# A decoder step on one core: operations re-ordered at six places, last sums and one evacuation split

## The chip, the cores and the metric

The kernel runs on one core of a Trainium2 chip. The metric is device microseconds of one execution. The engines are named as the profile names them: PE is TensorE (matmul), PEld its weight loads, DVE is VectorE, ACT is ScalarE, POOL is GpSimd, SP is SyncE, which issues most DMAs.

## The reference

One inference step of a hybrid decoder layer for 512 prompt rows and 64 sample rows (8 samples of 8 rows), all of width 1024, in float32:

```python
u = rms(x) * g_pre_mix;  proj = u @ w_in          # z, xbc, dt, q, k, v, ig, fg, og
xbc = silu(causal_conv(xbc, conv_w));  dt = softplus(dt + bias)
y = ssd_scan(xs, dt, a, bm, cm, h0)               # Mamba-2 heads, chunks, cumulative sums, exp
h = mlstm_scan(q, k, v, ig, logf, c0, n0, m0)     # stabilised mLSTM heads
x = x + rms(concat(y_gated, h_gated) @ w_out) * g_post_mix
x = x + rms(cross_attention(rms(x) * g_pre_x, mem_k, mem_v) @ w_xo) * g_post_x
u = rms(x) * g_pre_ffn
x = x + rms((silu(u @ w_gate) * (u @ w_up)) @ w_down) * g_post_ffn
```

It also returns the memory's keys and values, and the new states of the convolution, the SSM and the mLSTM for both groups.

## The kernel before, in words

The activations are kept transposed, features on the 128 partitions, the T = 576 rows of both groups in the free dimension. Most products are made in three matmuls: weights and activations are each split into a high part (a cast to a shorter float) and a low part (the rest), and `gemm` (L201 to L212) issues for each block k of 128 features high x high (L208), high weights x low activations (L209) and low weights x high activations (L211). A tile of output has two halves (`HALVES`: 256 and 320 columns). Weights come in by DMA as 128x1024 floats (`split_w`, L178): ScalarE casts the high part, VectorE subtracts it for the low part, or ScalarE writes the negated high part and a GpSimd DMA adds the original on top.

The work goes through stages. (1) The input projection, 36 tiles of weights; tiles 1 to 12 feed the convolution, and between them VectorE and ScalarE work on the gates' rows (`r1`, `r2`: cumulated logs, maxima), which PE turns into columns with ten small transposes (L586 to L594), copied by ScalarE to `CT` (L591, L595); two products with `CT` follow (L597, L604). (2) The SSD scan (`ssd_prompt`): per pair of heads two decay matrices, each made by a product (L669), additions on VectorE (L672), an exponential on ScalarE (L674, collected in `exps`, 16 in all) and a product on VectorE (L675), then 16 small matmuls (L682). PE's time is filled with the mLSTM's values (`values`, L840 on): two groups of two heads, whose last chunk of 64 sample rows is stacked on both halves of the partitions, copied by ScalarE (L877), summed by VectorE (L878) and scaled by ScalarE (L879). Then come the mLSTM scan, the output gates, and the output projection. (3) Cross-attention, and its output projection `xo` (L1539 on): tiles 0, 1 and 2 are computed around the last head, with their evacuation (a square for the norm, L270, and a scaled copy, L1560, both on ScalarE) kept back until tile 3's weights have been cast. The three PSUM banks of the pool `g` rotate: tile 3 takes that of tile 0. (4) The feed-forward part, with seven products in place of eight for each 2x2 block of weights and rows (`Seven`, `Pair` for gate and up, `Down`): VectorE builds sums and differences of weight tiles in `sw` and others, and `parts2` (L1867) casts the sum `sw` to high and low. `Down` (768 columns of weights, eight of them in two groups) accumulates on `f2`. (5) A last chunk of six blocks of the down projection without that scheme (`down_chunk`, `w_of`, L2158): second halves of all eight output tiles (order 6, 7, 0, 1, ... 5), where the first three start with four blocks while the last gate products are still being made (`last.late()`, products L1935, cast to `hh` and `hl` by `Plain.put`, L2138). (6) The end (L2178 on): the eight first halves, six steps each, with the second half's norm and output beside them; then squares, sums over features by products with a column of ones (`root`, L2181), a root on ScalarE, transposes of the result to token rows (`f_rows`), and the last additions and stores.

What sets the order: in most of the kernel a build-time scheduler orders the instructions of each engine by priority (`tc.high_priority`) and by a simulated timeline (`schedule_with_timeline_sim`, L113); `tc.issue_after(x)` makes the instructions of the block that run on the engine of `x` come behind `x` in that engine's queue, without a semaphore. From the attention's output projection to the first pair, and at the end, the order is written out: `at_(p, fn)` puts a step at place p, and `tc.manual_schedule` issues the steps sorted by place. At the end, half-tile step k of tile j stands at j + k/6, its evacuation `evac0` at j + 1.03, the transposes of tile rows at 7.35 and 8.2, the sums `root` at 8.4, the last transposes at 8.7. Engines run their own queue in order; SP's queue issues loads in order, each waiting for its buffer (`raw` has two buffers in the pool `weights`, `rawx` two in the pool `ffn`).

Of the kernel before, what the change touches and what calls it, by code (L numbers as in the profile page):

```python
# [11 lines left out]
F32 = mybir.dt.float32  # L12
F32R = mybir.dt.float32r
BF16 = mybir.dt.bfloat16
AF = mybir.ActivationFunctionType
# [100 lines left out]
def build(nc, tc, ctx, I, O):  # L116
# [52 lines left out]

    loads, casts, accs = [], [], []  # L170

# [5 lines left out]

    def split_w(src, n=1024, cut=CUT, acc=False, pool=None, to=None, raw=None):  # L178
# [7 lines left out]
        casts.append(A.copy(hi[:, :n], raw[:, :n]))  # L186
        for e, a, b in ((V, 0, cut), (G, cut, n)):
            if b > a and e is G and acc:

                A.activation(lo[:, a:b], hi[:, a:b].bitcast(F32), AF.Copy, scale=-1.0)  # L190
                accs.append(G.dma_start(lo[:, a:b], src[:, a:b], accum_op=ALU.add))  # L191
            elif b > a:
                e.tensor_tensor(lo[:, a:b], raw[:, a:b], hi[:, a:b].bitcast(F32), op=ALU.subtract)  # L193
        return hi, lo

    def split(hi, lo, src, eng=None, cast=None):
        c = (cast or A.copy)(hi, src)  # L197
        (eng or V).tensor_tensor(lo, src, hi.bitcast(F32), op=ALU.subtract)  # L198
        return c

    def gemm(ps, units, xh, xl, t0, n, k0=0, k1=None, order=None, late=0):  # L201


        tiles = [(hi[:, j * P:(j + 1) * P], lo[:, j * P:(j + 1) * P]) for hi, lo, nk in units for j in range(nk)]
        order = order or range(len(tiles))
        for i, k in list(enumerate(order))[k0:k1]:
            (wh, wl), ah, al = tiles[k], xh(k, t0, n), xl(k, t0, n)
            mm(ps, wh, ah, start=i == 0, stop=False)  # L208
            mm(ps, wh, al, start=False, stop=False)  # L209
            for c in range(late) if i == late - 1 else [i] if i >= late else ():  # L210
                m = mm(ps, tiles[order[c]][1], xh(order[c], t0, n), start=False, stop=c == len(tiles) - 1)  # L211
        return m  # L212
# [55 lines left out]
    def add_sq(pool, ssq, src, j, w=T, eng=None, t0=0, q=None):  # L268
        if j == 0:
            A.activation(ssq[:, t0:t0 + w], src, AF.Square)  # L270
# [314 lines left out]

    with tc.high_priority(offset=1000):  # L586
        psc = MP("ps_ct")
# [252 lines left out]
    def values(g):  # L840
# [15 lines left out]
        def products(u, c, first, last):  # L856
# [18 lines left out]
            if n == TS:  # L875
                o = vts[:TS, 2 * g:2 * g + 2, 0:256]
                A.copy(o, p2[TS:P])  # L877
                V.tensor_tensor(o, o, p2[:TS], op=ALU.add)  # L878
# [660 lines left out]
    def xo(j, i, pool=None):  # L1539
# [11 lines left out]
        def step(k0, k1):  # L1551
# [4 lines left out]
            evx.append(None)  # L1556

            def out():
                add_sq(ph, ssq, ps, j if i == 0 else XO1.index(j), n, t0=t0)
                evx[at_e] = A.activation(f[:, j, t0:t0 + n], ps, AF.Copy, scale=PAR("g_postx", j))  # L1560

# [266 lines left out]
    class Seven:  # L1828
# [85 lines left out]
    class Pair(Seven):  # L1914
# [8 lines left out]
        def done(s, a, i, ps, more=None):  # L1923
# [7 lines left out]
            if more is not None:  # L1931
                t_ = ct[:, 1, :]
                V.tensor_tensor(t_, ps, more, op=ALU.add)
                ps = t_
            V.tensor_tensor(g, g, ps, op=ALU.mult)  # L1935
            s.put(s.j + a, a, i, g)
# [197 lines left out]
    class Plain:  # L2134
# [3 lines left out]
        def put(s, j, a, i, g):  # L2138
            split(*[t_[:, j % 8, E[i]] for t_ in s.b], g)

# [39 lines left out]

    def root(name, terms, chunks):  # L2181

        n, ps = len(chunks), B0("ps_ss")
        for m, (t_, b) in enumerate(terms):
            for c, (t0, _) in enumerate(chunks):
                mm(ps[:, c:c + 1], t_[:, t0 - b:t0 - b + P], ones, start=m == 0 and c == 0, stop=m == len(terms) - 1, skip_group_check=True)
        v, y, a, r = few[:] if n == 3 else [fp.tile([P, n], F32, name=name + k) for k in ("_v", "_y", "_a", "_r")]
# [24 lines left out]
    def evac0(j):  # L2212
        fj = f2[:, j, 0:256]
        V.tensor_tensor(fj, fj, tail[j], op=ALU.add)
        if j:
            squares[j] = ph.tile([P, 320], F32, name="sq", tag="sq", bufs=2)[:, :256]
        A.activation(squares[j] if j else ssqf[:, 0:256], fj, AF.Square)
        if j < 7:
# [67 lines left out]
    for i in range(4):  # L2286
# [131 lines left out]
```

## Time and profile before

| | |
|---|---|
| median of 3 runs | 1079.36 us (1078.49 to 1079.89) |
| the profiled execution | 1077.81 us |
| its span, first to last instruction | 1075.9 us |
| granted TensorE clock | 0.997 |
| PE idle by its own marks, 0 to 100 us of the span | 2.11 us |
| 220 to 250 us | 0.30 us |
| 620 to 645 us | 0.13 us |
| 842 to 943 us, 943 to 1020 us | 0.05 us each |
| 1020 to 1048 us | 0.09 us |
| from the last `ps_dn` product, 1067.12 us, to the end | 6.93 of 8.78 us |

A row of the timeline gives start, duration, engine, line of the kernel, operation, output and input by the program's names, shapes and a count of merged instructions; a bracket tells how long the engine was idle before it and who released it. A group's row gives line, engine, operation, names, shapes and count, then busy time in us, the mean of one in ns, and the idle time ahead. Matmuls are pipelined: their rows overlap.

### The profile page before, as it was taken

The page shows a single profiled execution, that of the slowest core. Times are in us where ns is not written, and L with a number is a line of the kernel's source. Part 1 is how long each engine was busy: PE and PEld are TensorE (multiplying, and loading weights), DVE is VectorE, ACT ScalarE, POOL GpSimd, SP SyncE. Part 2 cuts the span into 40 slices and gives each one's busy share as a digit, 9 for nine tenths or more (in the row PEclk, how much of TensorE's full clock was granted, in tenths as well). Part 3 has the DMA queues.
Part 4 walks back from the last instruction along what each step waited for, and adds up shares of the span by engine and source line. Part 5 has one row for each costly group of instructions (what it writes and reads, how often), then busy time and mean ns, then how long its engine had stood idle before and what let it go on. Part 6 is the DMA issues. An engine that isn't in the chain of part 4 may idle for free.

```text
span 1075.9 us, 20705 instructions
## 1 busy us (share of the span) xinstructions
PE 1066.2 (99%) x8122; PEld 1013.8 (94%) x8122; DVE 751.8 (70%) x1509; ACT 607.6 (56%) x1094; POOL 231.7 (22%) x305
## 2 busy tenths in 40 slices
PE   9999999999999999999999999999999999999997
PEld 8999887778999999999999989999999999999997
DVE  6897775758877775559655555766467887787556
ACT  7778522345654556556555445545566566656653
POOL 1454543213213111000154201100011111111000
PEclk9999999999999999999999999999999999999998
DMA  6785544435655349643468775743476687578532
GB/s 208 177 161 131 157 138 166 147 85 172 197 148 150 107 131 341 234 168 116 143 212 286 266 256 171 252 127 94 133 180 142 156 201 165 116 190 185 128 132 89
DMA packets 58966, 181.76 MB, mean 169 GB/s; under 512 B 6604, under 2 KB 12108, under 8 KB 58356
## 3 DMA queue, kind: packets, MB, share of 16 engines
q1 hardware_dynamic: 42884, 138.22, 38.4%
q0 software_dynamic: 15408, 41.43, 19.3%
q8 instruction: 64, 1.05, 0.4%
q10 hardware_dynamic: 576, 0.79, 0.2%
q14 instruction: 34, 0.28, 0.1%
HBM read 159.75 MB, written 20.65 MB: 168 GB/s over the span
## 4 chain that ended last, share of the span: by engine, by line
PE 95%; DVE 3%; ACT 1%; issue 1%; DMA 0%; SPq 0%; DVEq 0%; ACTq 0%
PE ps_in L208 6%; PE ps_in L211 6%; PE ps_in L209 6%; PE ps_v L854 5%; PE ps_o L211 3%; PE ps_g L1910 3%; PE ps_g L1909 3%; PE ps_o L209 3%; PE ps_g L1911 3%; PE ps_o L208 3%; PE ps_u L1910 3%; PE ps_u L1911 3%; PE ps_u L1909 3%; PE ps_dn L1909 2%; PE ps_dn L1910 2%; PE ps_dn L1911 2%
## 5 line engine op out<-in xcount | busy, mean ns | idle before, releaser
L208 PE MATMUL ps_in<-uh,whi 128*128 128x320 f32 (+1 forms) x544 | 161.7, 297 | 0.0
L211 PE MATMUL ps_in<-uh,wlo 128*128 128x320 f32 (+1 forms) x544 | 161.7, 298 | 0.0
L209 PE MATMUL ps_in<-ul,whi 128*128 128x320 f32 (+1 forms) x544 | 161.0, 296 | 0.0
L186 ACT CAST whi<-raw 128x1024 fp32r<-128x1024 f32 (+1 forms) x104 | 105.3, 1014 | 94.3 <-PE ps_in L209 27.7
L193 DVE TENSOR_TENSOR wlo<-raw,whi 128x1024 fp32r<-128x1024 f32 (+2 forms) x97 | 94.7, 978 | 59.6 <-ACT whi L186 58.7
L211 PEld LDWEIGHTS ps_in<-uh,wlo 128*128 128x128 f32 x544 | 102.1, 188 | 2.0 <-issue 1.3
L208 PEld LDWEIGHTS ps_in<-uh,whi 128*128 128x128 f32 x544 | 102.3, 188 | 1.7 <-issue 0.8
L209 PEld LDWEIGHTS ps_in<-ul,whi 128*128 128x128 f32 x544 | 102.3, 188 | 0.4
L191 POOL DMA_DIRECT2D wlo<-win x31 | 27.0, 872 | 78.0 <-ACT wlo L190 65.5
L1909 PE MATMUL ps_g<-b,whi 128*128 128x288 f32 x144 | 42.5, 295 | 0.0
L1910 PE MATMUL ps_g<-b,whi 128*128 128x288 f32 x144 | 42.4, 295 | 0.0
L1910 PE MATMUL ps_u<-b,whi 128*128 128x288 f32 x144 | 42.2, 294 | 0.0
L1909 PE MATMUL ps_u<-b,whi 128*128 128x288 f32 x144 | 42.2, 294 | 0.0
L1882 ACT CAST whi<-rawx 128x1024 fp32r<-128x1024 f32 (+1 forms) x26 | 25.7, 988 | 27.6 <-PE ps_dn L1910 13.7
L198 DVE TENSOR_TENSOR wlo<-sw,whi 128x1024 fp32r<-128x1024 f32 (+1 forms) x26 | 29.6, 1140 | 15.0 <-ACT whi L197 14.9
L208 PE MATMUL ps_xo<-qh,whi 128*128 128x288 f32 x128 | 38.4, 302 | 0.1
L209 PE MATMUL ps_xo<-ql,whi 128*128 128x288 f32 x128 | 37.7, 296 | 0.0
L211 PE MATMUL ps_o<-mixm_h,wlo 128*128 128x256 f32 (+1 forms) x128 | 37.7, 295 | 0.0
L209 PE MATMUL ps_o<-mixm_l,whi 128*128 128x256 f32 (+1 forms) x128 | 37.5, 293 | 0.0
L211 PE MATMUL ps_xq<-u2h,wlo 128*128 128x320 f32 (+1 forms) x128 | 37.5, 294 | 0.0
L211 PE MATMUL ps_o<-mixs_h,wlo 128*128 128x320 f32 (+1 forms) x128 | 37.4, 292 | 0.0
L209 PE MATMUL ps_xq<-u2l,whi 128*128 128x320 f32 (+1 forms) x128 | 37.4, 294 | 0.0
(770 smaller groups left out, 3842.2 us busy)
## 6 DMA issues: line engine op xcount, KB each, us to landing
raw<-win SPq DMA_DIRECT2D x35, 512.0 KB, 4.2
raw<-wout SPq DMA_DIRECT2D x17, 512.0 KB, 4.4
raw<-wxq SPq DMA_DIRECT2D x13, 512.0 KB, 3.9
raw<-wgate SPq DMA_DIRECT2D x13, 512.0 KB, 3.5
raw<-wup SPq DMA_DIRECT2D x13, 512.0 KB, 4.8
wlo<-win POOLq DMA_DIRECT2D x24, 256.0 KB, 5.1
kva<-vc SPq DMA_DIRECT2D x11, 512.0 KB, 6.6
raw<-wv SPq DMA_DIRECT2D x10, 512.0 KB, 4.3
```

Of the source, the lines that this page charges most:

```text
L186: casts.append(A.copy(hi[:, :n], raw[:, :n]))
L191: accs.append(G.dma_start(lo[:, a:b], src[:, a:b], accum_op=ALU.add))
L193: e.tensor_tensor(lo[:, a:b], raw[:, a:b], hi[:, a:b].bitcast(F32), op=ALU.subtract)
L198: (eng or V).tensor_tensor(lo, src, hi.bitcast(F32), op=ALU.subtract)
L208: mm(ps, wh, ah, start=i == 0, stop=False)
L209: mm(ps, wh, al, start=False, stop=False)
L211: m = mm(ps, tiles[order[c]][1], xh(order[c], t0, n), start=False, stop=c == len(tiles) - 1)
L854: mm(ps, a, b, skip_group_check=True, **kw)
L1882: A.copy(s.h3[:, s.all], s.r2[:, s.all])
L1909: mm(ps, wh, b[0][k], start=start and k == 0, stop=False, skip_group_check=True)
L1910: mm(ps, wh, b[1][k], start=False, stop=False, skip_group_check=True)
L1911: m = mm(ps, wl, b[0][k], start=False, stop=k == nk - 1, skip_group_check=True)
```

## The change

Six places change.

1. Gates: the block of transposes and of products with `CT` is issued, on PE, after `products[140]`; `products` collects the L209 matmul of every step of `gemm`.
2. Values: in the second group the copy L877 is issued, on ScalarE, after `exps[13]`, the 14th exponential of the scan.
3. `xo`: the scaled evacuation of tile (0, 0) is done by VectorE as soon as the tile is complete; only its square stays with those kept back.
4. `parts2`: for `Down`, the cast is made in two halves, the second half of the columns (`LB`) first; the subtraction stays whole.
5. `w_of`: `split_w` with a place of its own (`to`) now issues its cast behind a given ScalarE instruction and its subtraction behind a given VectorE instruction and in pieces. Tile 0's subtraction is in two pieces; tile 2's is behind the last gate product; tile 2 is fetched before tile 1, whose subtraction follows that of 2; casts of 3 and 4 are behind the last cast of hidden rows; tile 4 is loaded to `sw`.
6. The end: the sums for the first half (`pf0`) are made in two parts, that of `ssqf` at place 7.6, that of the last tile's squares at 8.4; the last tile's evacuation and square go in two halves of 128 columns.

```diff
+    def split_w(..., piece=None, behind=None, after=None):
         if to:
-            split(*to, raw[:, :n])
+            with tc.issue_after(after.ins) if after else ExitStack():
+                A.copy(to[0], raw[:, :n])
+            with tc.issue_after(behind.ins) if behind else ExitStack():
+                for a in range(0, n, piece or n):
+                    b = a + (piece or n)
+                    wlows.append(V.tensor_tensor(to[1][:, a:b], raw[:, a:b], to[0][:, a:b].bitcast(F32), op=ALU.subtract))
             return to
...
-            mm(ps, wh, al, start=False, stop=False)
+            products.append(mm(ps, wh, al, start=False, stop=False))
...
-    with tc.high_priority(offset=1000):
+    with tc.issue_after(products[140].ins), tc.high_priority(offset=1000):
         psc = MP("ps_ct")
...
-                A.copy(o, p2[TS:P])
+                with tc.issue_after(exps[13].ins) if g else ExitStack():
+                    A.copy(o, p2[TS:P])
                 V.tensor_tensor(o, o, p2[:TS], op=ALU.add)
...
+            if (j, i) == (0, 0):
+                V.tensor_scalar(f[:, j, t0:t0 + n], ps, PAR("g_postx", j), None, op0=ALU.mult)
             def out():
-                add_sq(ph, ssq, ps, j if i == 0 else XO1.index(j), n, t0=t0)
-                evx[at_e] = A.activation(f[:, j, t0:t0 + n], ps, AF.Copy, scale=PAR("g_postx", j))
+                e = add_sq(ph, ssq, ps, j if i == 0 else XO1.index(j), n, t0=t0)
+                evx[at_e] = e if (j, i) == (0, 0) else A.activation(f[:, j, t0:t0 + n], ps, AF.Copy, scale=PAR("g_postx", j))
...
-            split(s.h2[:, s.all], s.l2[:, s.all], sw[:, s.all])
+            for c in (s.LB, s.LA) if isinstance(s, Down) else [s.all]:
+                A.copy(s.h2[:, c], sw[:, c])
+            V.tensor_tensor(s.l2[:, s.all], sw[:, s.all], s.h2[:, s.all].bitcast(F32), op=ALU.subtract)
...
     def w_of(j):
         if j not in kept:
+            behind = {}
+            if j == 2:
+                behind[2] = last.product
+            if j == 1:
+                w_of(2)
+                behind[1] = wlows[-1]
...
-            raw = fp.tile([P, 1024], F32, name="rawx", tag="rawx", bufs=2) if j % 2 else None
-            kept[j] = split_w(src, 768, 768, raw=raw, to=None if j > 4 else (wdh[:, j, :], wdl[:, j, :]))
+            raw = fp.tile([P, 1024], F32, name="rawx", tag="rawx", bufs=2) if j % 2 else sw if j == 4 else None
+            kept[j] = split_w(src, 768, 768, raw=raw, to=None if j > 4 else (wdh[:, j, :], wdl[:, j, :]),
+                              piece=384 if j == 0 else None, behind=behind.get(j), after=stores[-1].cast if 2 < j < 5 else None)
...
     def evac0(j):
-        V.tensor_tensor(fj, fj, tail[j], op=ALU.add)
...
-        A.activation(squares[j] if j else ssqf[:, 0:256], fj, AF.Square)
+        o = squares[j] if j else ssqf[:, 0:256]
+        for c in [slice(0, 256)] if j < 7 else [slice(0, P), slice(P, 256)]:
+            V.tensor_tensor(fj[:, c], fj[:, c], tail[j][:, c], op=ALU.add)
+            A.activation(o[:, c], fj[:, c], AF.Square)
...
-    at_(8.4, lambda: root("pf0", [(ssqf, 0), (squares[7], 0)], HCHUNKS[0]))
+    at_(7.6, lambda: sums("pf0", [(ssqf, 0)], HCHUNKS[0], True, False))
+    at_(8.4, lambda: root("pf0", [(squares[7], 0)], HCHUNKS[0], False))
```

`last.product` is the last L1935 product of the last `Pair`, `stores[-1].cast` the last cast of `Plain.put`; both are only kept for these references. `sums` holds the products of the former `root` (L2186), with start and stop passed in.

More of the change, by code (lines that the diff above doesn't have):

```diff
@@ L167, in build @@
     ident, ones = C32("ident"), C32("ones")
-    loads, casts, accs = [], [], []
+    loads, casts, accs, wlows = [], [], [], []
     def hi_lo(pool=None):
@@ L176, in hi_lo, with split_w @@
         return hi, (pool or wp).tile([P, 1024], F32R, name="wlo", tag="wlo", bufs=NWX if pool else 3)
-    def split_w(src, n=1024, cut=CUT, acc=False, pool=None, to=None, raw=None):
+    def split_w(src, n=1024, cut=CUT, acc=False, pool=None, to=None, raw=None, piece=None, behind=None, after=None):
         if raw is None:
@@ L199, in split @@
         return c
+    products = []
     def gemm(ps, units, xh, xl, t0, n, k0=0, k1=None, order=None, late=0):
@@ L269, in add_sq @@
         if j == 0:
-            A.activation(ssq[:, t0:t0 + w], src, AF.Square)
+            return A.activation(ssq[:, t0:t0 + w], src, AF.Square)
         else:
@@ L1934, in done @@
                 ps = t_
-            V.tensor_tensor(g, g, ps, op=ALU.mult)
+            s.product = V.tensor_tensor(g, g, ps, op=ALU.mult)
             s.put(s.j + a, a, i, g)
@@ L2138, in put @@
         def put(s, j, a, i, g):
-            split(*[t_[:, j % 8, E[i]] for t_ in s.b], g)
+            s.cast = split(*[t_[:, j % 8, E[i]] for t_ in s.b], g)
     for n_, j0 in enumerate((10, 16)):
@@ L2179, in build, with sums, root @@
     tail, squares = {}, {}
-    def root(name, terms, chunks):
-        n, ps = len(chunks), B0("ps_ss")
+    def sums(name, terms, chunks, first, last):
+        if first:
+            tail["ss", name] = B0("ps_ss")
         for m, (t_, b) in enumerate(terms):
             for c, (t0, _) in enumerate(chunks):
-                mm(ps[:, c:c + 1], t_[:, t0 - b:t0 - b + P], ones, start=m == 0 and c == 0, stop=m == len(terms) - 1, skip_group_check=True)
+                mm(tail["ss", name][:, c:c + 1], t_[:, t0 - b:t0 - b + P], ones, start=first and m == 0 and c == 0,
+                   stop=last and m == len(terms) - 1, skip_group_check=True)
+    def root(name, terms, chunks, first=True):
+        sums(name, terms, chunks, first, True)
+        n, ps = len(chunks), tail["ss", name]
         v, y, a, r = few[:] if n == 3 else [fp.tile([P, n], F32, name=name + k) for k in ("_v", "_y", "_a", "_r")]
```

## The prediction

> **What bounds the kernel now.** I read the engine line of the page first, then the list of what each engine waited for, then the timeline of TensorE (PE) around each place that the diff touches.
>
> ```profile
> PE 1066.2 (99%) x8122; PEld 1013.8 (94%) x8122; DVE 751.8 (70%) x1509; ACT 607.6 (56%) x1094; POOL 231.7 (22%) x305
> ```
>
> PE is busy for 1066.2 of 1075.9 us. No matmul is added or dropped by the diff, so all it can win is time in which PE stands still, and that is little. I measure a stand-still by spacing, not by the idle mark. The chain of waits gives what one matmul adds when nothing is waited for, at 320, 288 (six together) and 256 columns:
>
> ```profile
> 82.03 0.15 PE ps_in L208
> ```
> ```profile
> 636.92 0.79 PE ps_xo L211 x6
> ```
> ```profile
> 1061.07 0.11 PE ps_dn L211
> ```
>
> That is 0.145, 0.13 and 0.115 us, while the timeline shows each for 0.28 to 0.31 us; so a wait can hide under the modelled end of the matmul before it. [...]
>
> **The change part by part.** Each place below is a wait of PE in the trace; the gain is the start after the wait less the start before it less one spacing.
>
> *Gates (L586).* The ten small transposes of `r1` and `r2` are to be issued after `products[140]` on PE. Counting the `gemm` steps in program order, 136 to 143 are the second half of the input tile of j = 9, in which the transposes stand now, after the first matmul of k = 3; number 140 is the L209 matmul of k = 4.
>
> ```profile
> 79.10 0.31 PE L208 MATMUL ps_in<-uh,whi 128*128 128x320 f32 x1
> 79.62 0.28 PE L589 MATMUL ps_ct<-c,r 100*128 100x100 f32 x1 [0.21 <-ACT r L567]
> ```
> ```profile
> 83.72 0.49 ACT L591 COPY CT<-ps_ct 128x416 f32<-128x416 f32 x1
> ```
>
> PE could go on at 79.10 + 0.145 = 79.25 and starts at 79.62: 0.37 us (the idle mark says 0.21). Four matmuls (L209 and L211 of k = 3, L208 and L209 of k = 4) are put in front: 4 x 0.145 = 0.58 us, more than the wait. The transposes then start at 79.83 and end 0.2 us later than now; the copy on ScalarE that reads them starts only at 83.72, held up by its queue and not by PE, so that hides. Gain 0.21 to 0.37, I take **0.37**.
>
> *Values (L877).* The copy of the samples' half of the second values group goes behind the 14th exponential on ScalarE.
>
> ```profile
> 236.88 0.59 ACT L877 COPY vts<-ps_v 64x512 f32<-64x512 f32 x1
> 237.37 0.63 ACT L674 ACTIVATE lm<-lm 128x512 f32<-128x512 f32 x1
> ```
> ```profile
> 237.50 0.68 DVE L878 TENSOR_TENSOR vts<-vts,ps_v 64x512 f32<-64x512 f32 x1
> 238.11 0.68 DVE L675 TENSOR_TENSOR lm<-lm,cbs 128x512 f32<-128x512 f32 x1
> ```
> ```profile
> 238.35 0.28 PE L211 MATMUL ps_in<-uh,wlo 128*128 128x256 f32 x1
> 238.93 0.33 PE L682 MATMUL ps_yi<-lm,xdt 128*64 128x128 f32 x2 [0.30 <-DVE lm L675]
> ```
>
> Now the copy runs right ahead of the 14th exponential, and its sum L878 between the two products L675. After the change the 14th exponential takes the place at 236.88 and its product that at 237.50, ending at 238.18; PE is free at 238.47. Spacing 0.46, idle mark 0.30; a change of operand costs a little too, so I take **0.40**. Behind the copy on ScalarE are the cast of a later weight tile and L879, half a microsecond later; the PSUM bank that the copy frees is not the next one taken, since three rotate. I cost that at nothing; if the bank were next, PE would wait up to the copy's 0.59.
>
> *Output projection of the attention (L1560).* The scaled evacuation of tile (0, 0) goes from ScalarE to VectorE and is no longer kept back; the bank of tile 0, which tile 3 takes, then waits only for the square.
>
> ```profile
> 634.21 0.41 ACT L270 ACTIVATE ssqxo<-ps_xo 128x288 f32<-128x288 f32 x1
> 634.51 0.49 ACT L1560 ACTIVATE f_xo<-ps_xo,par 128x288 f32<-128x288 f32 x1
> ```
> ```profile
> 634.34 1.23 DVE L193 TENSOR_TENSOR wlo<-raw,whi 128x1024 fp32r<-128x1024 f32 x1 [2.30 <-ACT whi L186]
> ```
> ```profile
> 634.64 0.29 PE L211 MATMUL ps_xo<-qh,wlo 128*128 128x288 f32 x1
> 635.06 0.40 PE L208 MATMUL ps_xo<-qh,whi 128*128 128x288 f32 x1
> ```
>
> The square ends at 634.62, and PE is free at 634.77: **0.29** gained, with 0.15 to spare. The new VectorE instruction falls in the 2.30 us that VectorE idles before 634.34; without that cover it would cost about the 0.49 of the instruction that it replaces. Bounds 0 and 0.29.
>
> *Down weights (`parts2`).* The cast of 768 columns becomes two of 384, the half that the next product uses first.
>
> ```profile
> 842.38 0.84 ACT L197 CAST whi<-sw 128x768 fp32r<-128x768 f32 x1 [0.65 <-PE ps_dn L1910]
> ```
> ```profile
> 842.92 0.29 PE L1911 MATMUL ps_dn<-te,wlo 128*128 128x288 f32 x1
> 843.27 0.41 PE L1909 MATMUL ps_dn<-hh,whi 128*128 128x288 f32 x1
> ```
> ```profile
> 942.90 0.29 PE L1911 MATMUL ps_dn<-te,wlo 128*128 128x288 f32 x1
> 943.24 0.41 PE L1909 MATMUL ps_dn<-hh,whi 128*128 128x288 f32 x1
> ```
> ```profile
> L197 ACT CAST whi<-sw 128x768 fp32r<-128x768 f32 x8 | 6.6, 828 | 1.3 <-PE ps_dn L1910 1.3
> L197 ACT CAST u3h<-d 128x384 fp32r<-128x384 f32 x8 | 4.1, 507 | 0.0
> ```
>
> PE waits 0.22 and 0.21 us, at the first tile of each of two groups. A half ends at 842.38 + 0.51 = 842.89, before PE is free (843.05): **0.43** gained. The price is 2 x 0.507 - 0.828 = 0.19 us of ScalarE, eight times, 1.5 us in all, on an engine that is busy 56% of the span; at the other six tiles PE does not wait for the cast. The Trainium skill (VectorE: DVE Perf Modes, The TRN2 errata) says that each VectorE or ScalarE instruction on SBUF pays a fixed extra latency and advises 512 elements or more; the trace agrees that there is such a part, with the 0.19 us; that speaks against this split and is a rival below.
>
> *Last down chunk (`w_of`).* The low part of weights 0 comes in two pieces; the low parts of 2 and then 1 go behind the last gate product on VectorE, the casts of 3 and 4 behind the last hidden cast on ScalarE; weights 4 get a buffer of their own.
>
> ```profile
> 1028.45 0.31 PE L209 MATMUL ps_dn<-hl,wdh 128*128 128x320 f32 x1
> 1028.80 0.41 PE L211 MATMUL ps_dn<-hh,wdl 128*128 128x320 f32 x1
> ```
> ```profile
> 1028.66 0.45 DVE L1933 TENSOR_TENSOR ct<-ps_u,ct 128x288 f32<-128x288 f32 x1
> 1029.03 0.95 DVE L198 TENSOR_TENSOR wdl<-rawx,wdh 128x768 fp32r<-128x768 f32 x1
> 1029.89 0.45 DVE L1935 TENSOR_TENSOR gt<-gt,ct 128x288 f32<-128x288 f32 x1
> ```
> ```profile
> 1029.86 0.95 ACT L197 CAST hh<-gt 128x288 fp32r<-128x288 f32 x2
> ```
> ```profile
> 1030.50 0.30 PE L209 MATMUL ps_dn<-hl,wdh 128*128 128x320 f32 x1
> 1030.86 0.41 PE L208 MATMUL ps_dn<-hh,whi 128*128 128x320 f32 x1
> ```
>
> PE waits 0.20 us for the low part of weights 0 (half of it is ready some 0.4 us earlier) and 0.21 us for the hidden cast, which waits for the product at 1029.89, which stands behind the 0.95 us low part of weights 1. With that part moved the product can start by about 1029.3, and the casts end before PE asks. I take **0.40** of 0.41. Behind the moved low parts wait PE's products with the low part of 1, now some 1.9 us after the product, about 1031.6; PE has the high parts of four tiles to do meanwhile. In SyncE's queue the load of 2 comes ahead of that of 1, which then waits with it for a buffer; I cost that at nothing, since all weights of the chunk but 4 and 5 have landed before the casts here. The load of 5, and the input behind it, leave later by the delay of the low part of 1; both are read only after the products of five more tiles. Lower end: if PE keeps its order and waits for low part 1, nothing is gained.
>
> *End.* The sums of squares that close the first half are split: the part of `ssqf` goes to place 7.6 of the written order, before the last two of six steps of the last tile; the last evacuation comes in two halves of 128 columns.
>
> ```profile
> 1067.61 0.51 PE L2186 MATMUL ps_ss<-c,ssqf 128*128 128x1 f32 x4
> 1068.09 0.61 PE L2186 MATMUL ps_ss<-c,sq 128*128 128x1 f32 x4
> ```
> ```profile
> 1068.09 0.38 PE L2186 MATMUL ps_ss<-c,sq 128*128 128x1 f32 x2
> ```
> ```profile
> 1067.16 0.42 DVE L2214 TENSOR_TENSOR f_ffn<-f_ffn,ps_dn 128x256 f32<-128x256 f32 x1 [2.09 <-PE ps_dn L211]
> ```
> ```profile
> 1067.62 0.42 ACT L2217 ACTIVATE sq<-f_ffn 128x256 f32<-128x256 f32 x1 [1.99 <-DVE f_ffn L2214]
> ```
>
> Now the `ssqf` part (1067.61 to 1068.09, 0.48 us) lies beside the evacuation and square, which end at 1068.04: it is hidden. Put ahead of the last steps it delays the last product, and so the evacuation, by up to 0.48. What comes back: of the two sums of squares only one is left after the last square; the first two of its four passes take 0.38 us, all four 0.61 (the same instructions in a shorter and a longer window of the timeline), so 0.23. The evacuation in halves overlaps add and square, but each half pays its start: between -0.21 (halves at half price) and +0.42 (each half at the price of the whole); I take nothing, between these, since the two engines overlap and neither is free of a start. The end is **0.25 later**, between 0 and 0.7.
>
> *Sum.* 0.37 + 0.40 + 0.29 + 0.43 + 0.40 = 1.89; less 0.25 is **1.64 us** off the profiled execution's 1077.81, which gives 1076.2. That execution lies 1.55 below the median 1079.36; I apply the difference to the median: **1077.7**. From the low ends (0.21 + 0.30 + 0 + 0.43 + 0 - 0.7) to the high ones (1.96 - 0) the forecast's own range is 1077.4 to 1079.1.
>
> **Rivals.**
> - *The end costs nothing:* the first sums slip in beside weight loads. For: PE's loads overlap. Against: the spacing of 0.48 above. 1079.36 - 1.89 = 1077.5.
> - *The waits move on, and the change does not do what it says:* gates, values and `w_of` only change an order that the scheduler fills in by its own clock; a new last waiter appears and these three give nothing. 1079.36 - 0.29 - 0.43 + 0.25 = 1078.9. For: at `w_of` three engines are within 0.3 us of each other. Against: the slack computed at each.
> - *Slower by the gates:* with the transposes later, the scheduler puts the copy of `ps_ct` (83.72 now) behind two casts of whole weight tiles, 1.01 us each by this group, and PE waits for it at the products L597 that read it.
>
> ```profile
> L186 ACT CAST whi<-raw 128x1024 fp32r<-128x1024 f32 (+1 forms) x104 | 105.3, 1014 | 94.3 <-PE ps_in L209 27.7
> ```
>
>   It decides where the copies end after PE has come to L597, which it does not wait for now; with 2.0 us of wait the time is 1079.36 - 1.64 + 2.0 = 1079.7. Against: ScalarE's queue has the copy late already, for reasons of its own.
> - *Slower by the halves:* if PE waited for the second half of the cast at all eight tiles, the eight extra 0.19 us would be on the path and the 0.43 lost: 1079.36 - 1.64 + 0.43 + 1.49 = 1079.6. By the Trainium skill (VectorE: DVE Perf Modes, The TRN2 errata) small pieces lose in this way. Against: two waits in eight now, and the first half is what is read first.
>
> **How the numbers follow.** Chances: forecast 0.58, free end 0.12, waits move on 0.19, slower by the gates 0.07, by the halves 0.04. 0.2% (2.2 us), about what a measurement of this kernel can tell from no change, puts the bounds at 1077.2 and 1081.5. The runs of before lie up to 0.9 us from their median; so of the forecast I count 0.14 beyond 1077.2 and of the free end 0.07: faster 0.21. Of the slower cases 0.04 may pass 1081.5. The rest, 0.75, is within 0.2%. The range takes the forecast's 1077.4 less 0.8 of scatter, and at the top the slower rivals' 1079.7 with a little: 1076.6 to 1079.9.
>
> **What would show it.** Right: after the change no spacing over 0.2 us before the first transposes, before the L682 matmuls that follow the values, before output tile 3, before the third product of the first down tile in each group, and in the last chunk; and a last evacuation that starts about 1.4 us earlier while the span ends about 1.6 us earlier. Wrong: one of these spacings is still there with another engine named, or the time from the last `ps_dn` matmul to the end shrinks by far more than 0.2 us.

## The result, and the profile after

The changed kernel takes 1077.03 us (median of 15 runs, 1076.16 to 1079.76); the kernel before took 1079.38 in the runs beside it (15 runs, 1078.05 to 1080.64). The ratio is 0.9981 with a 95% interval of 0.9973 to 0.9988, so 2.05 us less, between 1.3 and 2.9. Forecast were 1.64 less and a median of 1077.7. The change also ran a second time in the experiments: 0.9979 (0.9970 to 0.9988).

The profiled execution of the changed kernel is the longest of its 15 runs (1079.76, span 1078.0 us; the profile of before had 1077.81 and 1075.9). So the two spans must not be subtracted; they say that the change is slower. I compare instead the start of the same matmul in both traces, place by place. I call the difference of the two starts the shift. A shift that grows along the trace is time lost since the last place, one that shrinks is time won.

The engine line of the page first:

```profile
PE 1067.4 (99%) x8122; PEld 1015.4 (94%) x8122; DVE 752.3 (70%) x1512; ACT 607.7 (56%) x1102; POOL 231.7 (21%) x305
```

PE has as many matmuls as before and is as full; the gain is not to be seen in busy time. Now the places of the prediction, in the timeline of the changed kernel (start, duration, engine, line). Gates:

```profile
81.82 0.31 PE L216 MATMUL ps_in<-ul,whi 128*128 128x320 f32 x1
81.97 0.25 PE L596 MATMUL ps_ct<-c,r 100*128 100x100 f32 x1
```

The first transpose now starts 0.15 us after the matmul ahead of it, one spacing; before it was 0.52. Values:

```profile
238.24 1.14 ACT L681 ACTIVATE lm<-lm 128x512 f32<-128x512 f32 x2
238.90 1.29 DVE L682 TENSOR_TENSOR lm<-lm,cbs 128x512 f32<-128x512 f32 x2 [0.62 <-ACT lm L681]
240.17 0.28 PE L218 MATMUL ps_in<-uh,wlo 128*128 128x256 f32 x1
240.37 1.09 PE L689 MATMUL ps_yi<-lm,xdt 128*64 128x128 f32 x16
```

The two exponentials and the two products stand side by side, the second product ends at 240.19, and PE goes on after 0.20 instead of 0.58. Output projection:

```profile
636.68 0.52 DVE L1567 TENSOR_SCALAR f_xo<-ps_xo,par 128x288 f32<-128x288 f32 x1 [1.36 <-PE ps_xo L218]
637.92 0.29 PE L218 MATMUL ps_xo<-qh,wlo 128*128 128x288 f32 x1
638.05 0.30 PE L215 MATMUL ps_xo<-qh,whi 128*128 128x288 f32 x1
```

The scaling lies in VectorE's idle time, and tile 3 starts one spacing (0.13) after the matmul ahead of it; before it was 0.42. Down weights: the place that the prediction calls the first down tile of a group is the second of the group's four. In before the casts of `sw` for the first group start at 830.30, 842.38, 849.77 and 858.69, and the one at 842.38 is waited for; in the second group it is the one at 942.35. In the changed kernel:

```profile
845.17 0.93 ACT L1881 CAST whi<-sw 128x384 fp32r<-128x384 f32 x2 [0.65 <-PE ps_dn L1923]
845.72 0.29 PE L1924 MATMUL ps_dn<-te,wlo 128*128 128x288 f32 x1
845.85 0.29 PE L1922 MATMUL ps_dn<-hh,whi 128*128 128x288 f32 x1
845.98 0.29 PE L1923 MATMUL ps_dn<-hl,whi 128*128 128x288 f32 x1
846.15 0.40 PE L1922 MATMUL ps_dn<-hh,whi 128*128 128x288 f32 x1
846.39 0.29 PE L1923 MATMUL ps_dn<-hl,whi 128*128 128x288 f32 x1
```

The wait ahead of 845.85 is gone. A smaller one is left two products further: 846.15 comes 0.17 after 845.98, and the next start 0.24 after that, where 0.13 is the spacing. The cast's second half, which ends at 845.17 + 0.93 = 846.10, is what that product reads. Last down chunk:

```profile
1030.90 0.31 PE L216 MATMUL ps_dn<-hl,wdh 128*128 128x320 f32 x1
1031.05 0.31 PE L218 MATMUL ps_dn<-hh,wdl 128*128 128x320 f32 x1
1032.65 0.31 PE L218 MATMUL ps_dn<-hh,wdl 128*128 128x320 f32 x1
1032.80 0.45 PE L215 MATMUL ps_dn<-hh,whi 128*128 128x320 f32 x2
```

Both spacings of 0.35 and 0.36 are 0.15 now. The end, with VectorE's `pf_v` as the first reader of the sums:

```profile
1068.11 0.50 PE L2207 MATMUL ps_ss<-c,ssqf 128*128 128x1 f32 x4
1068.47 0.36 PE L215 MATMUL ps_dn<-hh,whi 128*128 128x256 f32 x1
1069.13 0.28 PE L218 MATMUL ps_dn<-hh,wlo 128*128 128x256 f32 x1
1070.14 0.61 PE L2207 MATMUL ps_ss<-c,sq 128*128 128x1 f32 x4
1070.78 0.16 DVE L2217 TENSOR_SCALAR pf_v<-ps_ss 128x2 f32<-128x2 f32 x1 [0.45 <-PE ps_ss L2207]
```

The early sums stand between two down products (0.36 to the next one, then 0.20 instead of 0.12: 0.45 in all by the shift). From the last down product to the last sums it is 1.01 us; before it was 1068.09 - 1066.84 = 1.25. The end is 0.22 later.

Where the longer span comes from is seen in three places that the diff does not touch, and at which all engines have the same order in both kernels: the first input products (2.13 us later than in the trace of before), 0.5 us between 424 and 445 us, and 1.2 us at 580 us, where a weight load lands late:

```profile
579.82 1.05 ACT L191 CAST whi<-raw 128x1024 fp32r<-128x1024 f32 x1 [1.70 <-DMA raw<-wmv]
581.64 0.39 PE L843 MATMUL ps_v<-wlo,memhl 128*128 128x256 f32 x1 [0.22 <-DVE wlo L198]
```

### The profile page after: what moved, and what is told of

Read it like the earlier page. It is cut to its first block, busy times and chain, and to the rows that moved or that the text cites. A ratio compares the mean times of both kernels' runs of the same rounds, so it can differ in the third digit from the quotient of the medians.

```text
span 1078.0 us, 20720 instructions
## 1 busy us (share of the span) xinstructions
PE 1067.4 (99%) x8122; PEld 1015.4 (94%) x8122; DVE 752.3 (70%) x1512; ACT 607.7 (56%) x1102; POOL 231.7 (21%) x305
## 4 chain that ended last, share of the span: by engine, by line
PE 94%; DMA 3%; ACT 1%; DVE 1%; POOL 1%; issue 1%; SPq 0%; DVEq 0%; ACTq 0%; POOLq 0%
PE ps_in L215 7%; PE ps_in L218 7%; PE ps_in L216 7%; PE ps_v L861 5%; PE ps_g L1923 3%; PE ps_u L1923 3%; PE ps_g L1922 3%; PE ps_u L1924 3%; PE ps_g L1924 3%; PE ps_u L1922 3%; PE ps_dn L1922 2%; PE ps_dn L1924 2%; PE ps_dn L1923 2%; PE ps_dn L215 2%; PE ps_o L218 2%; PE ps_o L215 2%
## 5 line engine op out<-in xcount | busy, mean ns | idle before, releaser
L218 PE MATMUL ps_in<-uh,wlo 128*128 128x320 f32 (+1 forms) x544 | 161.7, 298 | 0.0
L191 ACT CAST whi<-raw 128x1024 fp32r<-128x1024 f32 (+1 forms) x104 | 105.4, 1014 | 96.7 <-PE ps_in L216 30.7
L218 PEld LDWEIGHTS ps_in<-uh,wlo 128*128 128x128 f32 x544 | 102.1, 188 | 1.9 <-issue 1.3
L1872 ACT CAST whi<-raw 128x1024 fp32r<-128x1024 f32 (+1 forms) x26 | 25.6, 985 | 23.3 <-PE ps_g L1923 11.8
L218 PE MATMUL ps_o<-mixm_h,wlo 128*128 128x256 f32 (+1 forms) x128 | 37.7, 295 | 0.0
L215 PE MATMUL ps_o<-mixs_h,whi 128*128 128x320 f32 (+1 forms) x128 | 37.5, 293 | 0.1
L218 PE MATMUL ps_xq<-u2h,wlo 128*128 128x320 f32 (+1 forms) x128 | 37.5, 294 | 0.0
```

## The table of shifts

All traces of this study, each against the trace of before. A shift is a kernel's start of a matmul less that of the same matmul in before, as the median over the matched matmuls of a stretch beside the place; an entry is the shift behind the place less the shift ahead of it, so a negative one is a gain. An example from rows on show: the L211 product at 1028.80 in before is the L218 product at 1031.05 here, a shift of 2.25, and the one ahead, at 1028.45 and 1030.90, has 2.45; so 0.20 was won between these two. "Load" is not a shift but the median time from issue to landing of the two input weight loads issued between 225 and 238 us. Entries within 0.04 of zero are shown as 0; the stretches between the places, not shown, hold 0.15 at most.

```
trace            start  gates  values  behind  load  249-560 560-629  xo   down1  down2  w_of   end
after             2.13  -0.30   -0.38    0.08   4.4     0.54  1.23  -0.39  -0.18  -0.18  -0.62   0.23
after_again       0.83  -0.35   -0.37    0.08   4.2     1.20  0     -0.39  -0.18  -0.18  -0.62   0.22
old_tail          0.73  -0.34   -0.37    0.08   3.6     0     0     -0.39  -0.18  -0.17  -0.62   0
old_tail_again   -0.16  -0.32   -0.37    0.08   4.2     0.06  0     -0.39  -0.18  -0.18  -0.62   0
late_sums         2.63  -0.35   -0.38    0.09   3.5     0.62  0.99  -0.39  -0.18  -0.18  -0.62  -0.13
by_rows           2.05  -0.32   -0.38    0.09   3.6     0.74  0     -0.39  -0.30  -0.29  -0.62   0
rows_no_values    0.52  -0.34   -0.11    0      4.1     0     0.19  -0.39  -0.30  -0.29  -0.62   0
tail_alone        2.08   0      -0.38    0      3.7     0.49  0      0      0      0      0      0.22
w_of_alone        0.45   0      -0.38    0      3.6     1.17  0.39   0      0      0     -0.62   0
gates_values      0.86  -0.35   -0.36    0.09   4.3     0     0.07   0      0      0      0      0
xo_halves         2.07   0      -0.38    0      3.7     0     1.26  -0.39  -0.18  -0.18   0      0
gates_139         2.66  -0.12   -0.09    0      4.1     0     0.16   0      0      0      0      0
halves_swapped    0.80   0      -0.37    0      3.6     0     0.38   0     -0.19  -0.18   0      0
```

How to read it: gates, xo, down1, down2, w_of and end follow the kernel, row by row, to within 0.05 us. Start, 249-560 (with the delay between 424 and 445) and 560-629 (with the one at 580) do not follow it: kernels with the same order there have 0 or over 1 us. Values is the odd column: kernels without that part show its gain too. It is taken up in the last experiment.

## The experiments

`gates_139`, `halves_swapped`, `late_sums` and `rows_no_values` were executed once each, for the trace; no time of theirs is compared.

**The changed kernel again** (`after_again`, no edit).

> The changed kernel once more, unaltered. The trace of the changed kernel holds three delays that lie at no place of the diff: 2.3 us on the first input products, 0.5 us between 424 and 445 us, 1.2 us at 580 us; instruction orders there are the same. Theory (these belong to one execution): in this trace at least the 1.2 us at 580 is gone, and the profiled execution is nearer the median; time about 1077.1 +- 0.8. Rival (they come from the change, by a shifted DMA): they are there again in the same size. The places of the diff show the same gains in both cases: gates 0.36, values 0.38 with 0.10 lost at once behind, xo 0.37, halves 0.18 twice, last down chunk 0.62; 0.22 lost at the end.

Measured: 1077.04 us, ratio to before 0.9979 (0.9970 to 0.9988). The delay at 580 is gone, the one between 424 and 445 is larger (1.20), the start costs 0.83. The places of the diff are the same to 0.05. The three delays belong to an execution and not to the change.

**The end of before put back** (`old_tail`, twice).

```diff
-    at_(7.6, lambda: sums("pf0", [(ssqf, 0)], HCHUNKS[0], True, False))
-    at_(8.4, lambda: root("pf0", [(squares[7], 0)], HCHUNKS[0], False))
+    at_(8.4, lambda: root("pf0", [(ssqf, 0), (squares[7], 0)], HCHUNKS[0]))
...
-        for c in [slice(0, 256)] if j < 7 else [slice(0, P), slice(P, 256)]:
-            V.tensor_tensor(fj[:, c], fj[:, c], tail[j][:, c], op=ALU.add)
-            A.activation(o[:, c], fj[:, c], AF.Square)
+        V.tensor_tensor(fj, fj, tail[j], op=ALU.add)
+        A.activation(squares[j] if j else ssqf[:, 0:256], fj, AF.Square)
```

> The changed kernel with the end of the kernel before (sums of squares together behind the last tile, last evacuation whole). Theory (PE runs the early sums on the path: 0.45 paid before the last two steps, 0.23 given back): the first pf_v comes 1.89 us after the last down product instead of 1.65, the last product comes 0.45 earlier, and the time is 0.22 below the changed kernel, about 1076.8 (ratio to before 0.9976). Rival 1 (the end costs nothing): same as the changed kernel within 0.05. Rival 2 (the halves of the evacuation gain more than the sums cost): 0.2 slower.

> The changed kernel with the end of the kernel before, once more, beside the one with the other cut on the same chip. Theory: 1.5 to 2.0 below before by the places in the trace (0.36 gates, 0.37 output projection, 0.36 halves, 0.62 last down chunk, minus 0.1 to plus 0.3 values), ratio 0.9981 to 0.9986. Rival (there is a gain that no place in the trace shows): 3 us again, ratio 0.997.

Measured: 0.9970 (0.9959 to 0.9982, median 1076.49) and, on the second occasion, 0.9986 (0.9977 to 0.9995, median 1077.24). The trace of the second:

```profile
1064.78 0.28 PE L218 MATMUL ps_dn<-hh,wlo 128*128 128x256 f32 x1
1065.55 0.50 PE L2206 MATMUL ps_ss<-c,ssqf 128*128 128x1 f32 x4
1066.02 0.61 PE L2206 MATMUL ps_ss<-c,sq 128*128 128x1 f32 x4
1066.66 0.16 DVE L2210 TENSOR_SCALAR pf_v<-ps_ss 128x2 f32<-128x2 f32 x1 [0.76 <-PE ps_ss L2206]
```

`pf_v` comes 1.88 us after the last product, as the theory had it, and the end column is 0: the new end costs 0.22 by the trace. The times can't show so little: the two intervals are some 2 us wide. The 3 us of the first occasion did not come again, and the second interval (0.5 to 2.5 us less) holds the sum of the places, so a gain outside them is not shown.

**The new end alone** (`tail_alone`: the kernel before with the edits to `sums`, `root`, `evac0` and the written order).

> The kernel before with the new end alone (early sums, last evacuation in halves). Theory: 0.22 slower than before, about 1079.6: last product 0.45 later, 0.23 returned between it and the first pf_v. Rival (the end costs nothing or gains): the last product 0 to 0.1 later and the time equal or up to 0.25 less.

Measured: ratio 0.9998 (0.9988 to 1.0008); shift at the end 0.22 later. That is the theory's figure in the trace; the time agrees but would agree with none, too.

**Early sums taken back, halves of the evacuation kept** (`late_sums`: only the two `at_` lines of the diff above).

> The changed kernel with the sums of squares together behind the last tile as before, the last evacuation still in halves. Theory (with the sums late PE is busy until 1.25 us after the last product, and the second half of the square is there by 1.16): first pf_v 1.89 us after the last down product, as in the kernel before; the halves give nothing there. Rival (the halves gain by themselves): first pf_v at most 1.8 us after the last down product.

```profile
1069.15 0.28 PE L218 MATMUL ps_dn<-hh,wlo 128*128 128x256 f32 x1
1069.92 0.50 PE L2207 MATMUL ps_ss<-c,ssqf 128*128 128x1 f32 x4
1070.29 0.58 PE L2207 MATMUL ps_ss<-c,sq 128*128 128x1 f32 x4
1070.91 0.16 DVE L2217 TENSOR_SCALAR pf_v<-ps_ss 128x2 f32<-128x2 f32 x1 [0.57 <-PE ps_ss L2207]
```

`pf_v` comes 1.76 us after the last product, so the rival holds and my theory falls: PE was not busy until 1.25. The `ssqf` sums take 0.37 here and 0.47 in the old end, because there PE, after them, waits 0.1 us for the square to end. With halves, PE can begin on the first one. So the two edits at the end have opposite signs: the halves win 0.12 (1.88 less 1.76; 0.13 by the shift), and the early sums, with the halves there, lose 0.35 (from -0.13 to 0.22). Early sums with a whole evacuation were not run. Of the three ends that ran, this one, late sums with halves, is the shortest.

**The last down chunk alone** (`w_of_alone`: the kernel before with the edits to `split_w`, `done`, `put` and `w_of`).

> The kernel before with the part on the last down chunk alone. Theory (each wait of PE costs its 0.20 and another 0.1 of a wider spacing behind it): the starts behind 1031 us come 0.62 earlier, in two steps of 0.31, and the time is about 1078.8 (ratio 0.9994). Rival (the prediction's count: 0.20 a wait): 0.40 to 0.41 earlier. Rival (the gain came from elsewhere, by the moved order of the groups before): under 0.2.

Measured: ratio 0.9990 (0.9981 to 0.9999), 1.1 us less with an interval of 0.1 to 2.0. The shift falls by 0.62, as in each trace with this part. So the prediction's 0.40 was too small. What it left out is seen in before, in the timeline of PE behind the first of the two waits:

```profile
1028.45 0.31 PE L209 MATMUL ps_dn<-hl,wdh 128*128 128x320 f32 x1
1028.80 0.41 PE L211 MATMUL ps_dn<-hh,wdl 128*128 128x320 f32 x1
1029.05 0.30 PE L208 MATMUL ps_dn<-hh,wdh 128*128 128x320 f32 x1
1029.19 0.31 PE L209 MATMUL ps_dn<-hl,wdh 128*128 128x320 f32 x1
```

The matmul that waited is shown with 0.41 instead of 0.31, and the one behind it starts 0.25 later instead of 0.145. A wait costs its own length (0.35 - 0.145 = 0.205) and 0.105 more behind it. Two of them make 0.62.

**Gates and values** (`gates_values`: the kernel before with the two edits at L586 and L877).

> The kernel before with the transposes of the gates further back and the values' copy behind the exponential. Theory: 0.36 at the gates and 0.38 at the values with 0.10 lost behind them within 10 us, 0.64 in all; time about 1078.7 (ratio 0.9994). Rival (the waits move on): the starts after 250 us come less than 0.3 earlier than those before 79 us would have them. Rival (the 0.10 behind belongs to the execution and not to the order): 0.74.

Measured: ratio 1.0000 (0.9991 to 1.0009). Gates -0.35, values -0.36, behind 0.09: 0.62 by the trace, against 0.64 expected. The time shows none of it, and its interval, up to 1.0 us less, still holds it.

**The transposes one matmul back instead of four** (`gates_139`: the kernel before, `products[139]` instead of `products[140]`).

> The kernel before with the transposes behind products[139] on PE, one matmul back instead of four. Theory (a wait of 0.37 for a fixed time on ScalarE, filled by matmuls of 0.145): 0.145 gained, about 0.22 of wait left ahead of the first transpose. Rival (the wait is not for a fixed time but follows the matmul in front, as by a shared port or a queue): the whole 0.37 is still there, or all of it is gone.

```profile
81.91 0.30 PE L211 MATMUL ps_in<-ul,whi 128*128 128x320 f32 x1
82.28 0.28 PE L591 MATMUL ps_ct<-c,r 100*128 100x100 f32 x1
```

One matmul in front leaves a start-to-start time of 0.37, so 0.225 of wait, where the theory had 0.22: each matmul put ahead covers its own 0.145. That fits a wait for a fixed time on ScalarE.

**Output projection and halves** (`xo_halves`: the kernel before with the edits at L1560 and in `parts2`).

> The kernel before with the evacuation on VectorE and the halves of the down weights alone. Theory: 0.37 at 635 us, 0.18 at 843 and 0.18 at 943, with a rest of 0.15 of wait at the third first-part product of each group's first down tile; 0.73 in all, time about 1078.6 (ratio 0.9993). Rival (the halves cost ScalarE time that PE meets): a start later by 0.1 or more at some other down tile of the two groups, or in the gate products, whose order the halves change.

Measured in the trace: -0.39 and twice -0.18, 0.75 in all, and no loss at any other down tile; the rival on ScalarE's time falls. In time: ratio 1.0005 (0.9996 to 1.0014), which does not hold the 0.9993 expected. The profiled execution has a late landing at 580 (1.26 us) that has nothing to do with the part; whether such delays fell more often into these eleven runs by chance is not settled. Added up, the ratios of the four kernels with a part each (`tail_alone`, `w_of_alone`, `gates_values`, `xo_halves`) come to 0.8 us less, give or take some 2.0, an estimate. So the times do not confirm the parts one by one; their sizes rest on the shifts.

**Halves in the other order** (`halves_swapped`: the kernel before with the edit in `parts2` alone and its two halves exchanged; the minus line is that of the changed kernel).

```diff
-            for c in (s.LB, s.LA) if isinstance(s, Down) else [s.all]:
+            for c in (s.LA, s.LB) if isinstance(s, Down) else [s.all]:
```

> The kernel before with the down weights' cast in two halves, but the half that PE reads second cast first. Every other order is that of the kernel with the right halves. Theory (the gain is the earlier end of the half that is read first): nothing gained, the wait at 843 and 943 is 0.22 or up to 0.1 longer. Rival (the gain of 0.18 comes from the order of the products, which the scheduler changes with either split): 0.18 at each is still gained.

```profile
843.95 0.29 PE L1913 MATMUL ps_dn<-te,wlo 128*128 128x288 f32 x1
844.08 0.29 PE L1911 MATMUL ps_dn<-hh,whi 128*128 128x288 f32 x1
844.21 0.29 PE L1912 MATMUL ps_dn<-hl,whi 128*128 128x288 f32 x1
844.38 0.40 PE L1911 MATMUL ps_dn<-hh,whi 128*128 128x288 f32 x1
```

The same 0.19 and 0.18 are won. In the built order of PE's instructions the first two products write another accumulator than with the other order: the scheduler puts first the product whose half is cast first. So the experiment did not hold the order still, as I had assumed; it shows that it does not matter which half comes first, as long as PE's order may follow.

**The cast cut by what PE reads** (`by_rows`: the kernel with the old end, another cut).

```diff
-            for c in (s.LB, s.LA) if isinstance(s, Down) else [s.all]:
-                A.copy(s.h2[:, c], sw[:, c])
+            if isinstance(s, Down):
+                h, w = [t_[:, s.all].rearrange("p (a k c) -> p a k c", a=2, c=P) for t_ in (s.h2, sw)]
+                A.copy(h[:, :, 0], w[:, :, 0])
+                A.copy(h[:, :, 1:3], w[:, :, 1:3])
+            else:
+                A.copy(s.h2[:, s.all], sw[:, s.all])
```

> The kernel with the end of the kernel before and all other parts of the change, with the down weights' cast cut another way: first the 2 x 128 columns that PE reads in its first two products, then the other 2 x 256. Theory (what is left of the wait, 0.04 and 0.11 of wider spacing behind it, is for the second half of 384): the starts behind 846 and behind 946 us come 0.15 earlier each than with the halves, 0.30 in all, with no spacing over 0.15 at the third product; time 0.30 below the kernel with the old end, about 0.5 below the changed kernel. Rival (the first piece now ends too late, a cast of 256 columns in two strided runs costing more than 0.5): the wait of 0.2 is back. Rival (the second piece is waited for further on): a new spacing over 0.2 within the next ten products.

```profile
844.06 0.41 ACT L1882 CAST whi<-sw 128x256 fp32r<-128x256 f32 x1 [0.65 <-PE ps_dn L1927]
844.38 0.62 ACT L1883 CAST whi<-sw 128x512 fp32r<-128x512 f32 x1
844.61 0.29 PE L1928 MATMUL ps_dn<-te,wlo 128*128 128x288 f32 x1
844.74 0.30 PE L1926 MATMUL ps_dn<-hh,whi 128*128 128x288 f32 x1
844.87 0.30 PE L1927 MATMUL ps_dn<-hl,whi 128*128 128x288 f32 x1
845.01 0.30 PE L1926 MATMUL ps_dn<-hh,whi 128*128 128x288 f32 x1
```

No spacing over 0.14 is left, and the two groups win 0.30 and 0.29 instead of 0.18 each; 0.23 more in all, against 0.30 expected. Time: ratio 0.9985 (0.9975 to 0.9994), beside 0.9986 of the same kernel with halves on the same chip; 0.23 us is below what these runs tell apart. It is, with the old end, the version with the largest sum of places that ran; `late_sums`' end together with this cut was not run.

**Without the part on the values** (`rows_no_values`: `by_rows` with the copy back in its place).

> The first kernel of this set without the part on the values' copy. Theory (whether PE waits at the values is set by the landing of the two input weight loads issued ahead of them): if their median landing is 4.1 us or more, PE waits 0.38 ahead of the first decay products of that stage, as in two of the traces without this part; if it is 3.7 or less, there is no wait, as in four; the 0.08 to 0.10 lost about 8 us later with this part is gone in both cases. Rival (the part is needed whatever the landing): a wait of 0.3 or more at a landing of 3.7 or less.

The rows of PE's timeline, and the landing from the view of the transfers between 225 and 238 us, here and in `tail_alone`:

```profile
238.58 0.28 PE L218 MATMUL ps_in<-uh,wlo 128*128 128x256 f32 x1
239.06 0.40 PE L689 MATMUL ps_yi<-lm,xdt 128*64 128x128 f32 x3 [0.20 <-DVE lm L682]
```
```profile
raw<-win SPq DMA_DIRECT2D x2, 512.0 KB, 4.1
```
```profile
raw<-win SPq DMA_DIRECT2D x2, 512.0 KB, 3.7
```

The landing was 4.1, and PE waits: start to start 0.48, against 0.20 in the changed kernel, which does not wait, so 0.28 (0.38 was expected; 0.28 also in `gates_139`, 0.38 in before). The seven traces without this part divide as the theory says: landings of 4.1 to 4.3 with a wait (before, `gates_139`, `rows_no_values`), 3.6 or 3.7 without one (`tail_alone`, `w_of_alone`, `xo_halves`, `halves_swapped`). In the seven with the part there is no wait, at landings from 3.5 to 4.4. The chain is: the load lands, ScalarE casts it, and the exponentials stand behind that cast in ScalarE's queue. Of the two loads it is the first that differs: it took 4.8 to 5.1 us in the seven traces with a late landing and 3.5 to 3.8 in the others, the second 3.5 to 3.7 in all. In before it took 4.9, in the two other late traces without the part 4.8, which fits the 0.10 between their waits. That the landing decides is shown by the division and by this chain; that nothing else varies with it was not tried.

The 0.08 to 0.09 lost behind is in all seven traces with the part and in none without. The moved sum is not what is waited for there, since VectorE stands idle ahead of the next decay matrices. In before and in the changed kernel:

```profile
243.52 0.39 PE L669 MATMUL ps_l<-cumst,c 80*128 80x512 bf16 x1
243.95 0.35 DVE L672 SCALAR_TENSOR_TENSOR lm<-ps_l,ncum,c 128x128 f32<-128x128 f32 x1 [2.24 <-PE ps_l L669]
```
```profile
245.11 0.39 PE L676 MATMUL ps_l<-cumst,c 80*128 80x512 bf16 x1
245.53 0.35 DVE L679 SCALAR_TENSOR_TENSOR lm<-ps_l,ncum,c 128x128 f32<-128x128 f32 x1 [2.09 <-PE ps_l L676]
```

The shift ahead is 1.44, and here it is 1.59 on PE and 1.58 on VectorE. In the built order the first product `ps_l` stands one matmul further back in the traces with the part, behind a high x high one. The additions start 0.14 later, and the products with the decay matrices behind them begin 0.08 to 0.09 later.

## Why the prediction came out right, step by step

*The sum* held, in part by luck: 1.64 less was forecast and 2.05 (1.3 to 2.9) measured. By the places of the profiled execution it is 0.30 + 0.38 - 0.08 + 0.39 + 0.36 + 0.62 - 0.23 = 1.74. The forecast's method (spacing instead of the idle mark, and the wait that is left) found all the places, and the rivals fall: the end costs 0.22; each place shows a shift; the copy of `ps_ct` (86.03 to 86.52) is done before its reader on PE starts at 86.76; and no other down tile waits. The single terms were less good than the sum: values, down weights and gates were put too high, the output projection and the last down chunk too low, and these errors cancel in part. With the 0.05 for the values that is worked out below, the places add up to some 1.5 for a mean execution, an estimate.

- *Gates, 0.37*: right at the place (a wait of 0.37 gone), and 0.30 to 0.35 by the shift some 10 us on, where PE's order moved a little too. The slope of 0.145 a matmul is seen in `gates_139` (0.12 by the shift).
- *Values, 0.40*: 0.28 to 0.38, in the traces with a late landing only, and the 0.08 to 0.09 lost behind was costed at nothing. Three of seven landings without the part were late: 3/7 x 0.31 (mean of 0.38, 0.28 and 0.28) - 0.08 = 0.05 us, an estimate for a mean execution. The step that failed is to take a wait of one profiled execution for one of the kernel: the row of the load's landing had to be set beside it.
- *Output projection, 0.29*: 0.39. The place and the cover were right (VectorE did it in idle time); the wider spacing behind the wait, 0.23 instead of 0.13 (635.06 to 635.29 in before), was left out.
- *Down weights, 0.43*: 0.36, of which that wider spacing is a part again. The wait is at the second tile of each group and not at the first, which changes neither the sum nor the mechanism. A rest of 0.15 at each group stayed, since the second half is asked for 0.26 us after the first. The price was over-estimated: two casts take 0.93 together, one whole 0.84, so 0.09 and not 0.19. The Trainium skill (VectorE: DVE Perf Modes, The TRN2 errata) advises large instructions because of a fixed latency in each; here, back to back on ScalarE, the second hides about half of its own, and PE never meets it.
- *Last down chunk, 0.40*: 0.62, the largest error within one pair of traces and the term that was mis-sized: 2 x 0.31 instead of 2 x 0.20. The order of the low parts held, and no new wait came.
- *End, 0.25 later*: 0.22 to 0.23. The cost of the early sums was right (0.45 of "up to 0.48"). That halves of the evacuation give nothing was wrong (0.12), and what the early sums return between the last product and `pf_v` was over-estimated by as much (0.11, with the halves there, instead of 0.23).

The result lies near the bound of 2.2 us between "within 0.2%" and "faster": 2.05 by the ratio, 2.35 by the medians. What no step had, beside the `ps_l` product that moved, was that the halves make the scheduler move PE's instructions in 34 places of its built order in the two groups; the shifts return to the same value behind each, so it costs nothing, but it was not foreseen.

## What to carry to other kernels

Where an engine is full, add up waits by the spacing of starts, and count both the wait and the wider spacing behind it; then ask of each wait whether a transfer's landing decides it, because then it belongs to some executions only. When gains are a fifth of the scatter, compare starts of the same instruction across traces, place by place, rather than spans or medians. And cut a cast at what its reader asks for first, not in the middle.

## What the runs showed of the hardware that was not expected

- Behind a matmul that waited, the next start came 0.10 to 0.11 us later than the spacing: 0.25 instead of 0.145 at 320 columns, 0.23 to 0.24 instead of 0.13 at 288. Such a gap is not found behind waits alone: it was 0.20 instead of 0.12 behind the down product that follows the early sums, where the trace shows no idle time.
- The same weight load of 512 KB landed in 3.5 to 3.8 us in seven executions and in 4.8 to 5.1 in seven others, with nothing in between; the load behind it took 3.5 to 3.7 in all fourteen.
- Executions differ by -0.2 to 2.7 us at the start and by up to 1.3 us in two later stretches, whichever kernel runs. One profile against one profile would have given the wrong sign here.
- A cast in two strided runs cost no more here than a contiguous one: 2 x 128 columns took 0.40 us in the mean and 2 x 256 took 0.62, where a straight line through the contiguous casts (0.51 for 384 columns, 0.83 for 768) gives 0.40 and 0.61, an estimate.
